# A trunk kernel on one core: a product moved inside each pair, one copy removed, stores moved to another queue

## The chip, the core and the metric

The kernel runs on one core of a Trainium2 chip. TensorE multiplies, VectorE and ScalarE work on tiles, GpSimd computes little here and issues DMAs, and SyncE only issues DMAs. Each engine takes its instructions from one queue in a fixed order, so an instruction that waits holds up all that stand behind it. The metric is the time of one execution in device microseconds, as a median of several.

## The reference

One layer of a decoder trunk is computed on x of 1024 positions by 1024 channels, all in float32. The parts that matter:

```
u    = layer_norm(x) * (1 + scale) + shift
proj = u @ w_in + b_in            # 1024 -> 12288 columns, split into 10 blocks
y_a  = (pool(a_v) @ pool_w) * pool_scale * silu(a_g)
y_b  = b_b * dwconv3(b_c * b_h) * silu(b_g)
h_c  = dwconv31(c_a * sigmoid(c_b))
y_c  = silu(layer_norm(h_c)) * silu(c_g)
m    = sum over k of sigmoid(merge_k) * (y_k @ w_branch[k])
out  = layer_norm(ALPHA * x + gate * (m @ w_out))
```

The pooling takes windows of 2, 4, 8 and 16 positions; dwconv31 is a causal convolution with 31 taps for each channel by itself. The layer norm of h_c runs over channels, so it needs the sum of all channel tiles.

## The kernel before

**Tiles.** Channels lie on the 128 partitions, so that a tile of 128 channels by 1024 positions is one buffer of 4 KB per partition. There are 37 such buffers (`BIG_SLOTS`), handed out by `slot()`. Each product of float32 matrices is made of three matmuls in the float32r format (`mm3`, line 134), because every operand is split into a high part (ScalarE) and a low part (VectorE). One half-tile product is 128x512.

**Jobs.** The work is a list of jobs. First come four plain jobs (two convolution tiles), then 46 pairs, each of which computes two blocks of 128 output columns together. A pair uses a scheme with seven block products in place of eight, named in `Pair.run` by their factors: A11 B11, A12 B21, S1 T1, S2 T2, S3 T3, S4 B22, A22 T4. Each has 12 matmuls. They use three PSUM banks: px takes A11 B11, then S2 T2, S3 T3 and A22 T4 on top of it, pz takes S1 T1 and then S4 B22, py takes A12 B21. In between, the content of a bank is copied or added into the results r1 and r2 by ScalarE (lines 525, 530, 534) and VectorE (528, 536, 538), and the next product into that bank waits for it. Six banks are there in all, so two pairs can be under way.

The pairs are of five kinds: `b` and `d` (branch B), `a` (pooling), `c` (convolution input), `cg` and `m` (gates, whose results are stored to DRAM). A `c` pair is put in after a fixed number of other pairs (`every`). After each job from the third on, `conv_step` issues six of the 30 taps that VectorE runs for each convolution tile (line 610); the 31st is ScalarE's start of the tile (606). When a tile h is done, it is stored, and it is added to a running sum; for the first tile the sum is a copy made by ScalarE (620).

**Merges.** Then follow 8 merge jobs z for branch B (48 matmuls each), with 4 pooling jobs among them, 8 merge jobs for branch A and 8 for branch C. A merge job needs its weights (SyncE's loads, split in lines 408 and 414), all eight y tiles of its branch (loaded by GpSimd's queue, split in 129 and 130) and a gate tile. The pooling jobs need pooled tiles (`a_load`) and produce sga tiles, which are stored as branch A's y. During the branch B merges the convolution's statistics are computed: the sum is split, the mean made, each tile is loaded again (hc), the mean is taken off, the tile is stored, and squares are added up (`c_square`). During the branch A merges branch C's y is computed from it (`c_y`) and stored. At the end comes the product with w_out and the last layer norm.

**Queues and order.** Loads of weights go through SyncE. Stores of intermediate tiles and their loads go through GpSimd's queue, as `store()` does unless it is given another queue. The order of instructions on each engine is not written out by hand, except for the start (`START`): a planner places them when the program is built, by the order of the code as priority and a model of durations. Extra edges of `after()` keep an instruction behind another in that plan.

Of the kernel before, what the change touches and what calls it, by code (L numbers as in the profile page):

```python
# [11 lines left out]
AF = mybir.ActivationFunctionType  # L12
# [7 lines left out]
NT = D // P  # L20
# [39 lines left out]
def kernel(  # L60
# [16 lines left out]
    nc = tc.nc  # L77
# [15 lines left out]
    LEFT, RIGHT = slice(0, HALF), slice(HALF, S)  # L93
    HALVES = (LEFT, RIGHT)

    def slot(name, dt=F32):
        return big.tile([P, D], dt, tag="big", name=name)
# [5 lines left out]
    def bank(name):  # L103
        return ps_main.tile([P, HALF], F32, tag="main", name=name)
# [92 lines left out]
    def vec(n, i):  # L197
        return vec_cols[:, base[n] + i : base[n] + i + 1]
# [195 lines left out]
    class Job:  # L394
# [41 lines left out]
        def run(self):  # L436
            if hasattr(self, "finished"):
                return
            if self.run_own is not None:
                self.run_own(self.w)  # L440
                return
            if not hasattr(self, "ps"):
                for k in range(NT):
                    for h in range(2):
                        self.part(k, h)
            self.after(self.ps)

    def bias(col):
        return bin_cols[:, col // P : col // P + 1]

    class Pair:
# [68 lines left out]
        def run(self):  # L520
            col1, col2 = self.cols
            px, pz = bank(f"px_{self.name}"), bank(f"pz_{self.name}")
            r1, r2 = slot(f"r1_{self.name}"), slot(f"r2_{self.name}")
            self.product(px, "A11", "B11", True)
            nc.scalar.activation(r1[:, LEFT], px, AF.Identity, bias=bias(col1))
            py = bank(f"py_{self.name}")
            self.product(py, "A12", "B21", True)
            nc.vector.tensor_add(r1[:, LEFT], py, r1[:, LEFT])
            self.product(pz, "S1", "T1", True)
            marks["pair"] = nc.scalar.activation(  # L530
                r2[:, RIGHT], pz, AF.Identity, bias=bias(col2)
            )
            self.product(px, "S2", "T2", False)
            nc.scalar.activation(r1[:, RIGHT], px, AF.Identity, bias=bias(col1))
            self.product(px, "S3", "T3", False)
            nc.vector.tensor_add(r2[:, RIGHT], px, r2[:, RIGHT])
            self.product(pz, "S4", "B22", False)
            nc.vector.tensor_add(r1[:, RIGHT], pz, r1[:, RIGHT])
            self.product(px, "A22", "T4", False)
            self.after(r1, px, r2)  # L540

    def store(dst, src, q=None):
        return (q or nc.gpsimd).dma_start(out=dst, in_=src)  # L543

    def dram_tiles(name, n):
        return [dram.tile([P, S], F32, name=f"{name}{j}") for j in range(n)]
# [15 lines left out]
    conv = {"n": 0, "sum": None}  # L562
# [36 lines left out]
    def conv_step(n):  # L599
        while n > 0 and conv_todo:  # L600
            item = conv_todo[0]
            j, g, h, s = item
            w = cfw_cols[:, (K31 - 1 - s) * NT + j : (K31 - 1 - s) * NT + j + 1]
            if s == 0:
                h = item[2] = slot(f"h{j}")
                ins = nc.scalar.activation(h, g, AF.Identity, bias=vec("cf_b", j), scale=w)  # L606
                if j == 0:
                    after(ins, marks["u"])
            else:
                nc.vector.scalar_tensor_tensor(  # L610
                    out=h[:, s:], in0=g[:, : S - s], scalar=w, in1=h[:, s:],
                    op0=ALU.mult, op1=ALU.add,
                )
                n -= 1
            item[3] = s + 1
            if s == K31 - 1:
                conv_todo.popleft()
                if conv["sum"] is None:
                    conv["sum"] = slot("hsum")
                    nc.scalar.copy(conv["sum"], h)  # L620
                else:
                    nc.vector.tensor_add(conv["sum"], conv["sum"], h)
                store(h_dram[j], h)
                conv["n"] += 1


    y_dram = [dram_tiles(f"y{b}_dram", NT) for b in range(3)]
# [25 lines left out]
    def a_load(g):  # L653
        for ct in (2 * g, 2 * g + 1):
            pooled[ct] = load_split(f"pool{ct}", pool_dram[ct], "split")
        for ct in (2 * g, 2 * g + 1):
            sg_a[ct] = slot(f"sga{ct}")
            after(nc.gpsimd.dma_start(out=sg_a[ct], in_=sga_dram[ct]), marks["split"])

    def a_pool(g):  # L660
        def run(w):
            for o in range(2):
                ct = 2 * g + o
                ps = [bank(f"pool_ps{ct}_{h}") for h in range(2)]
                for i in range(2):
                    for h in range(2):
                        ph, pl = pooled[2 * g + i]
                        ws = slice((2 * i + o) * P, (2 * i + o + 1) * P)
                        mm3(
                            ps[h], w[:, 0, ws], w[:, 1, ws], ph[:, HALVES[h]], pl[:, HALVES[h]],  # L670
                            i == 0, i == 1,
                        )
                t = sg_a.pop(ct)
                for h in range(2):
                    nc.vector.scalar_tensor_tensor(  # L675
                        out=t[:, HALVES[h]], in0=ps[h], scalar=vec("pool_scale", ct),
                        in1=t[:, HALVES[h]], op0=ALU.mult, op1=ALU.mult,
                    )
                store(y_dram[0][ct], t)

        jobs.append(Job(f"pool{g}", pool_w[0][g], None, None, run=run))

# [81 lines left out]
    c_dram = dram_tiles("c_dram", NT)  # L764
# [5 lines left out]
    def c_square(j):  # L770
        t = c_state.pop(("h", j))
        nc.vector.tensor_sub(t, t, c_state["mean"])
        store(c_dram[j], t)
        sq = slot(f"sq{j}")
        nc.scalar.activation(sq, t, AF.Square)
        if j == 0:
            c_state["q"] = sq
        else:
            nc.vector.tensor_add(c_state["q"], c_state["q"], sq)
# [28 lines left out]
    def c_y(ct):  # L808
        n, sg = c_state.pop(("y", ct))
        nc.vector.tensor_mul(n, n, c_state["rb"])  # L810
        nc.scalar.activation(
            n, n, AF.Silu, bias=vec("cf_ln_b", ct), scale=vec("cf_ln_g", ct)
        )
        nc.vector.tensor_mul(n, n, sg)
        store(y_dram[2][ct], n)


    y, m, m_hi, m_lo, g_in = {}, {}, {}, {}, {}
# [1 line left out]
    def y_load(b, k, mark):  # L820
        y[b, k] = load_split(f"y{b}_{k}", y_dram[b][k], mark)
# [35 lines left out]
    for b in (1, 0, 2):  # L857
        for i in range(NT // 2):
            light.append(
                lambda b=b, i=i: gates(  # L860
                    f"m{b}_{i}", C_M + b * D + 2 * i * P, AF.Sigmoid, g_dram[b][2 * i : 2 * i + 2],
                    nc.sync if (b, i) == (2, NT // 2 - 1) else None,
                )
            )
    heavy = [f for group in todo for f in group]
# [5 lines left out]
            order.append(light[li])  # L871
            li += 1
    order += light[li:]
    every = 6
    j = CLASSIC // 2
    for n, f in enumerate(order):
        if n % every == every - 1 and j < NT:
# [4 lines left out]
    n_proj = len(jobs)  # L882
# [14 lines left out]
    for op in LOADS.split():  # L897
        what, n = op[0], int(op[1:])
# [73 lines left out]
    for i, job in enumerate(jobs):  # L972
        ahead(i)
        if i >= n_proj and job.early is not None:
            job.early()
        job.run()
        if i == n_proj - 1:
            for k in range(NT):
                y_load(1, k, "pair")
        if i >= 2:  # L980
            conv_step(TAPS if i < n_proj - 1 else NT * K31)
        for f, args in hooks.get(i, ()):
            f(*args)
        if 8 <= i < 8 + NT:
            gate_row(i - 8)
        if n_proj <= i < n_proj + 8 and (i - n_proj) % 2 == 0:
            a_load((i - n_proj) // 2)
        if i == n_a - 2:
            marks["y0"] = marks["split"]
            for k in range(NT):  # L990
                y_load(0, k, "y0")
        if i == n_c - 2:
            marks["y2"] = marks["split"]
            for k in range(NT):
                y_load(2, k, "y2")
        if i == n_jobs - 3:
            gate_load()
            for d in range(NT - 2):
                m_hi[d], m_lo[d] = split_slots(f"m{d}", m[d])
        if i >= n_jobs - 2:  # L1000
            d = i - n_jobs + NT
            m_hi[d], m_lo[d] = split_slots(f"m{d}", m[d])
        if i >= n_jobs - 3:
            for k in ((0, 1), (2, 3, 4), (5, 6, 7))[i - n_jobs + 3]:
                wout_prep(k)
# [5 lines left out]
    for i in range(NT):  # L1011
# [4 lines left out]
        n = D // parts  # L1016
# [7 lines left out]
        for q, k in order:  # L1024
# [5 lines left out]
            if k == NT - 1:  # L1030
                t = slot(f"og{i}_{q}")[:, :n]
# [50 lines left out]
```

## Time and profile before

| what | value |
|---|---|
| median of 3 runs | 1385.55 us (1384.88 to 1387.03) |
| the profiled execution | 1386.24 us |
| its span, first to last instruction | 1384.5 us |
| mean granted TensorE clock in it | 0.986 |
| matmuls | 5893 |
| DMA, mean over the span | 136 GB/s |

The clock is the share of full speed that TensorE was granted. In the profile's rows a number like L134 is a line of the kernel, DVE is VectorE, ACT ScalarE, PE TensorE, POOL GpSimd, and SPq SyncE's queue. In a timeline each row has the start in us from the span's start, the duration in us, the engine, the line, what is written from what, and in brackets how long the engine was idle before it and what ended that. A row of a stretch has, for TensorE, its weight loads, VectorE, ScalarE and GpSimd, the busy time and in parentheses the number of instructions that began in it.

### The profile page before, as it was taken

To read this page: it belongs to the slowest core of one execution; us is meant where nothing else is said; L and a number is where in the kernel's file an instruction comes from. 1 tells how busy PE (TensorE), PEld (TensorE's weight loads), DVE (VectorE), ACT (ScalarE), POOL (GpSimd) and SP (SyncE) were. 2 spreads that over 40 slices of the span, in tenths; PEclk is the share of its full clock that TensorE was granted. 3 is DMA by queue.
4 is the path that set the end of the run, shared out by engine and by line. 5 is a ranking of instruction groups with operands and counts; after the bars stand their busy time and mean duration, and the time that the engine had idled before them with its cause. 6 is when DMAs were issued, how large, how long until landed. Compare 5 with 4: busy or idle time off the path is not lost. (4 is left out here: it accounts for less than half of the span.)

```text
span 1384.5 us, 15237 instructions
## 1 busy us (share of the span) xinstructions
PE 1330.3 (96%) x5893; PEld 1097.3 (79%) x5893; DVE 1099.0 (79%) x1292; ACT 527.5 (38%) x652; POOL 113.0 (8%) x220
## 2 busy tenths in 40 slices
PE   4999799999999999999999999999897999999997
PEld 3778688887888888888888888888685888888886
DVE  7999999999999589958975998699645657645576
ACT  6554244434443444435343543444422333313100
POOL 2000000000000000000000000000212232200010
PEclk9999999999999999999999999999998999999999
DMA  9511323443222313222342234224868979712332
GB/s 320 158 46 47 106 76 94 131 126 107 65 88 95 104 46 108 98 69 79 111 146 77 76 119 139 92 84 137 311 227 281 341 274 335 273 61 77 122 107 92
DMA packets 167949, 188.40 MB, mean 136 GB/s; under 512 B 6292, under 2 KB 138820, under 8 KB 167876
## 3 DMA queue, kind: packets, MB, share of 16 engines
q1 hardware_dynamic: 141936, 94.91, 23.1%
q0 software_dynamic: 25408, 92.29, 17.9%
q8 instruction: 46, 0.75, 0.2%
q10 hardware_dynamic: 532, 0.22, 0.1%
q14 instruction: 27, 0.22, 0.0%
HBM read 137.06 MB, written 50.34 MB: 135 GB/s over the span
## 5 line engine op out<-in xcount | busy, mean ns | idle before, releaser
L610 DVE SCALAR_TENSOR_TENSOR h<-r_c,cfw_cols,h 128x1023 f32<-128x1023 f32 (+9 forms) x180 | 226.9, 1261 | 5.5 <-ACT h L606 5.3
L610 DVE SCALAR_TENSOR_TENSOR h<-cs,cfw_cols,h 128x1023 f32<-128x1023 f32 (+29 forms) x60 | 75.8, 1263 | 1.3 <-ACT h L606 1.0
L832 DVE TENSOR_TENSOR g<-ps_z,g 128x512 f32<-128x512 f32 x48 | 31.7, 687 | 51.6 <-PE ps_z L134 51.1
L408 ACT ACTIVATE w_z<-raw_z 128x1024 fp32r<-128x1024 f32 x24 | 25.2, 1060 | 124.3 <-PE ps_z L134 62.3
L134 PE MATMUL ps_p<-u,w_p 128*128 128x512 f32 x192 | 48.8, 409 | 0.6 <-DVE u L346 0.6
L134 PEld LDWEIGHTS ps_p<-u,w_p 128*128 128x128 f32 x192 | 36.8, 196 | 8.8 <-DVE u L346 1.7
L414 DVE TENSOR_TENSOR w_z<-raw_z,w_z 128x1024 fp32r<-128x1024 f32 x24 | 29.1, 1220 | 14.6 <-ACT w_z L408 14.6
L543 POOL DMA_DIRECT2D g_dram<-r_m x22 | 11.7, 532 | 349.4 <-ACT r_m L718 238.1
L134 PE MATMUL py_m<-u,wa_m 128*128 128x512 f32 x144 | 36.2, 389 | 0.0
L134 PE MATMUL ps_z<-y_3h,w_z 128*128 128x512 f32 x96 | 34.0, 391 | 1.7 <-ACT y_3h L129 1.7
L134 PE MATMUL ps_z<-y_0h,w_z 128*128 128x512 f32 x96 | 35.4, 403 | 0.0
L134 PE MATMUL px_m<-u,wa_m 128*128 128x512 f32 x144 | 34.8, 389 | 0.0
L134 PE MATMUL pz_m<-u,wc_m 128*128 128x512 f32 x144 | 34.6, 389 | 0.0
L134 PE MATMUL ps_z<-y_1h,w_z 128*128 128x512 f32 x96 | 34.0, 389 | 0.0
L134 PE MATMUL ps_z<-y_2h,w_z 128*128 128x512 f32 x96 | 33.8, 389 | 0.0
L134 PE MATMUL ps_z<-y_4h,w_z 128*128 128x512 f32 x96 | 33.5, 389 | 0.0
L134 PE MATMUL ps_z<-y_7h,w_z 128*128 128x512 f32 x96 | 33.3, 389 | 0.0
L134 PE MATMUL ps_z<-y_6h,w_z 128*128 128x512 f32 x96 | 33.3, 389 | 0.0
L134 PE MATMUL ps_z<-y_5h,w_z 128*128 128x512 f32 x96 | 33.3, 389 | 0.0
L1032 DVE TENSOR_TENSOR og<-out_ps,gate_b 128x512 f32<-128x512 f32 (+1 forms) x18 | 11.1, 624 | 26.7 <-PE out_ps L134 13.4
L134 PE MATMUL px_m<-t_1h,wb_m 128*128 128x512 f32 x96 | 32.1, 389 | 0.0
L134 PE MATMUL pz_m<-t_0h,wb_m 128*128 128x512 f32 x96 | 31.5, 389 | 0.0
(567 smaller groups left out, 3879.7 us busy)
## 6 DMA issues: line engine op xcount, KB each, us to landing
raw_m<-in_w_in_dram SPq DMA_DIRECT2D x24, 512.0 KB, 4.0
raw_z<-in_w_branch_dram SPq DMA_DIRECT2D x24, 512.0 KB, 10.3
g<-g_dram POOLq DMA_DIRECT2D x24, 512.0 KB, 8.2
g_dram<-r_m POOLq DMA_DIRECT2D x22, 512.0 KB, 3.6
ada<-in_w_ada_dram SPq DMA_DIRECT2D x32, 256.0 KB, 6.4
raw_b<-in_w_in_dram SPq DMA_DIRECT2D x16, 512.0 KB, 4.0
raw_d<-in_w_in_dram SPq DMA_DIRECT2D x16, 512.0 KB, 4.0
raw_a<-in_w_in_dram SPq DMA_DIRECT2D x16, 512.0 KB, 4.0
```

Source lines behind the costliest of these rows:

```text
L134: nc.tensor.matmul(ps, w, r, start=start and n == 0, stop=stop and n == 2, skip_group_check=True)
L408: nc.scalar.activation(self.w[:, 0, : self.width], raw, AF.Identity)
L414: marks["split"] = nc.vector.tensor_tensor(out=lo, in0=raw, in1=f32(hi), op=ALU.subtract)
L543: return (q or nc.gpsimd).dma_start(out=dst, in_=src)
L610: nc.vector.scalar_tensor_tensor(out=h[:, s:], in0=g[:, : S - s], scalar=w, in1=h[:, s:], op0=ALU.mult, op1=ALU.add,)
L832: nc.vector.tensor_mul(g[:, HALVES[h]], ps[h], g[:, HALVES[h]])
L1032: nc.vector.tensor_mul(t, ps[q], final["gate"][:, sl])
```

## The change

S1 T1 moves behind S2 T2 in each pair, with its eviction. The first convolution tile becomes the running sum itself, without a copy. The stores of the branch A and branch C y tiles and of the centred convolution tiles go to SyncE's queue, on which the weights are loaded, and so do those of one more gate pair (the last two pairs of the last branch in place of the last one). A `c` pair comes after every fifth place in the list instead of every sixth. Each group of pooled tiles is requested one job earlier.

```
-            self.product(pz, "S1", "T1", True)
-            marks["pair"] = nc.scalar.activation(
-                r2[:, RIGHT], pz, AF.Identity, bias=bias(col2)
-            )
             self.product(px, "S2", "T2", False)
             nc.scalar.activation(r1[:, RIGHT], px, AF.Identity, bias=bias(col1))
+            self.product(pz, "S1", "T1", True)
+            marks["pair"] = nc.scalar.activation(
+                r2[:, RIGHT], pz, AF.Identity, bias=bias(col2)
+            )
             self.product(px, "S3", "T3", False)
...
                 if conv["sum"] is None:
-                    conv["sum"] = slot("hsum")
-                    nc.scalar.copy(conv["sum"], h)
+                    conv["sum"] = h
...
-                store(y_dram[0][ct], t)
+                store(y_dram[0][ct], t, nc.sync)
...
-        store(c_dram[j], t)
+        store(c_dram[j], t, nc.sync)
...
-        store(y_dram[2][ct], n)
+        store(y_dram[2][ct], n, nc.sync)
...
-                    nc.sync if (b, i) == (2, NT // 2 - 1) else None,
+                    nc.sync if b == 2 and i >= NT // 2 - 2 else None,
...
-    every = 6
+    every = 5
...
-        if n_proj <= i < n_proj + 8 and (i - n_proj) % 2 == 0:
-            a_load((i - n_proj) // 2)
+        if n_proj - 1 <= i < n_proj + 7 and (i - n_proj) % 2 == 1:
+            a_load((i - n_proj + 1) // 2)
```

Here `n_proj` is the number of jobs before the merges, 50.

More of the change, by code (lines that the diff above doesn't have):

```diff
@@ L528, in run @@
             nc.vector.tensor_add(r1[:, LEFT], py, r1[:, LEFT])
+            self.product(px, "S2", "T2", False)
+            nc.scalar.activation(r1[:, RIGHT], px, AF.Identity, bias=bias(col1))
             self.product(pz, "S1", "T1", True)
@@ L532, in run @@
             )
-            self.product(px, "S2", "T2", False)
-            nc.scalar.activation(r1[:, RIGHT], px, AF.Identity, bias=bias(col1))
             self.product(px, "S3", "T3", False)
```

## The prediction

> **What bounds the kernel now.** I read the page first, for which engine is the bound, then the waits of TensorE, then stretches of equal length, which price a wait together with what follows it.
>
> ```profile
> span 1384.5 us, 15237 instructions
> PE 1330.3 (96%) x5893; PEld 1097.3 (79%) x5893; DVE 1099.0 (79%) x1292; ACT 527.5 (38%) x652; POOL 113.0 (8%) x220
> ```
>
> TensorE is the bound. Only time in which it stands still, or runs at a lower clock, can be won, and no matmul is added or removed. The profiled execution took 1386.24 us for this span. These are its waits from 60 us to 1375 us (line waited for, total, times, longest):
>
> ```profile
> PE pool_ps L134 <- ACT pool6h L129: 10.2, 1, 10.2
> PE px_b L134 <- ACT r_b L525: 5.6, 1, 5.6
> PE pz_d L134 <- DVE wb_d L508: 2.4, 1, 2.4
> PE pool_ps L134 <- ACT pool0h L129: 1.7, 1, 1.7
> PE ps_z L134 <- ACT y_3h L129: 1.7, 1, 1.7
> PE px_b L134 <- DVE wc_b L508: 1.4, 1, 1.4
> PE ps_z L134 <- DVE y_3l L130: 0.5, 1, 0.5
> ```
>
> That is the whole list: 23.5 us, in four places. Stretches show more than the waits, because matmuls after a wait are slower (busy us and count of each engine, then the granted clock, the DMA share and GB/s):
>
> ```profile
> 160.00:180.00 20.00, 11.97 (x37) 8.88 (x37) 17.05 (x17) 7.19 (x9) 0.53 (x1) 0.74 0.16 63
> 180.00:200.00 20.00, 20.00 (x90) 16.57 (x89) 19.98 (x23) 5.61 (x7) 0.00 (x0) 1.00 0.14 35
> 200.00:300.00 100.00, 100.00 (x443) 82.81 (x442) 96.47 (x103) 44.95 (x55) 3.19 (x6) 1.00 0.39 120
> 400.00:500.00 100.00, 100.00 (x443) 82.84 (x442) 77.54 (x86) 44.63 (x54) 3.19 (x6) 1.00 0.29 93
> 980.00:1000.00 20.00, 16.06 (x58) 11.17 (x57) 12.04 (x12) 9.97 (x11) 3.17 (x6) 0.91 1.02 389
> 1040.00:1060.00 20.00, 9.83 (x40) 7.81 (x39) 10.13 (x11) 4.14 (x5) 6.04 (x12) 0.78 0.79 257
> 1060.00:1080.00 20.00, 20.00 (x86) 16.47 (x86) 13.85 (x15) 7.09 (x7) 4.50 (x9) 0.97 0.87 302
> ```
>
> A full stretch of 20 us starts 90 matmuls, 0.222 us each. The stretch at 160 starts 37: 53 missing, **11.8 us** (place A). At 980 there are 58: 32 missing, **7.1 us** (place C). At 1040 and 1060 there are 40 and 86: 54 missing, **12.0 us** (place D). The 1.4 us for wc_b, in the first pair, is place B. A, C and D together, 30.9 us, are all that this change could win outside B.
>
> **The change part by part.**
>
> *The running sum.* Place A, on ScalarE and TensorE:
>
> ```profile
> 171.86 1.04 ACT L620 COPY hsum<-h 128x1024 f32<-128x1024 f32 x1 [9.87 <-DVE h L610]
> 172.81 0.68 ACT L525 ACTIVATE r_b<-px_b,bin_cols 128x512 f32<-128x512 f32 x1
> 173.54 0.79 PE L134 MATMUL px_b<-t_1h,wb_b 128*128 128x512 f32 x1 [5.63 <-ACT r_b L525]
> ```
>
> The copy stands in ScalarE's queue and waits 9.87 us for the last tap of the first convolution tile. Behind it stands the eviction that S2 T2 of that pair (px_b<-t_1h) needs, so TensorE waits 5.63 us and ends 0.05 us after that eviction. The 2.4 us for wb_d just before it hang on the same knot: the held S2 T2 keeps its weights, so the next pair's arrive late. The change deletes the copy (1.04 us of ScalarE, which is free) and lets the tile itself be the sum; nothing else on ScalarE then waits for a tap. The addition of the second tile now also waits for the first tile's store, which goes out when that tile ends, 30 taps earlier: no cost. Gain at most 11.8 us, at least 0: VectorE ran its late taps during the stall (17.05 us busy of 20) and has only 0.02 + 3.53 us free from 180 to 300. If TensorE no longer pauses, taps fall further behind, and taps are the one VectorE work that TensorE does not wait for. I take 9.8, leaving 2 us for a split or eviction that comes late behind taps.
>
> *A c pair after every five others.* A convolution tile is 30 taps on VectorE, six per job, so five jobs. With one pair in seven jobs the chain starves, which is the hole in VectorE's row at 400 to 500 (77.54 against 96.47). With one in six it starves at one job only, and by the order the code builds, the last tile ends with job 42 of jobs 0 to 49 instead of in the last one. The number of taps is unchanged. It costs nothing by itself where TensorE was fully busy beside a VectorE at 96.47 of 100 us, which the row at 200 shows; without that cover it is the second rival. What it brings is at place C, on GpSimd's queue:
>
> ```profile
> 959.46 0.54 POOL L734 DMA_DIRECT2D y_0l<-y_dram  x1
> ...
> 971.49 0.54 POOL L543 DMA_DIRECT2D g_dram<-r_m  x1 [10.96 <-ACT r_m L557]
> 972.01 0.53 POOL L734 DMA_DIRECT2D y_2l<-y_dram  x1
> 975.10 0.54 POOL L543 DMA_DIRECT2D h_dram<-h  x1 [2.56 <-DVE h L610]
> 975.63 0.53 POOL L734 DMA_DIRECT2D y_3l<-y_dram  x1
> ...
> 985.85 0.73 PE L134 MATMUL ps_z<-y_3h,w_z 128*128 128x512 f32 x2 [1.67 <-ACT y_3h L129]
> ```
>
> The loads of the first merge's input stand behind a gate store (10.96 us waiting) and behind the last tile's store. The change takes away both: the third gate pair's two stores of the last branch move to the weight queue, and the last tile is done seven jobs sooner (84 matmuls each at 0.226 us, 133 us). y_2 can then be issued up to 11 us sooner and y_3 up to 3 us more than that. Both ends: 7.1 us if buffers are free as early as the queue, 0 if a buffer is what they wait for, since the pairs' operands hold most of the 37 buffers until the last products. The load of y_0 went out at 959, 16 us before the queue let y_3 go, so buffers do come free early: I take 5.5. The first pooling load now stands ahead of the first gate load, so that gate lands up to four loads later; its product waits in a bank, of which there are six: no cost.
>
> *Stores on the weight queue, pooling loads one job sooner.* Place D, on GpSimd's queue:
>
> ```profile
> 1044.40 0.54 POOL L543 DMA_DIRECT2D y_dram<-sga  x1 [13.01 <-DVE sga L675]
> 1046.25 1.05 POOL L768 DMA_DIRECT2D hc<-h_dram  x2
> 1047.29 0.53 POOL L734 DMA_DIRECT2D pool6l<-pool_dram  x1
> 1057.19 1.06 ACT L129 ACTIVATE pool6h<-pool6l 128x1024 fp32r<-128x1024 f32 x1 [7.94 <-DMA pool6l<-pool_dram]
> ```
>
> pool6l was issued behind two stores that waited for VectorE and behind two loads of convolution tiles, then took 9.9 us to land. In the changed code neither stands ahead of it: those stores are SyncE's, and the request comes one job sooner, before the hc loads. The queue stood idle from 1031.4 (1044.40 less 13.01); the load may go then, if its buffer is free. By the code I count 36 of 37 buffers then: 16 for y_1, 5 gate tiles, 12 for two pooling groups, 3 for the sum and its halves. Issued by 1037 it lands by 1047, where TensorE began to wait. Gain between 3.3 us (if it only takes the place of the first of these rows, 1047.29 against 1044.0, and lands as slowly) and 12.0; I take 10.9.
>
> What the 24 stores plus two gate stores cost on SyncE is the time for which weight loads stand behind a waiting store:
>
> ```profile
> POOL y_dram L543 <- DVE sga L675: 47.5, 6, 19.8
> 1012.58 0.37 SPq L386 DMA_DIRECT2D raw_z<-in_w_branch_dram  x1
> 1044.05 1.06 ACT L408 ACTIVATE w_z<-raw_z 128x1024 fp32r<-128x1024 f32 x1 [6.33 <-PE pool_ps L134]
> raw_z<-in_w_branch_dram SPq DMA_DIRECT2D x24, 512.0 KB, 10.3
> ```
>
> The weight load at 1012.58 is for the fifth merge job, whose split starts at 1044.05: 31.5 us, of which 10.3 to land, so 21 us in hand. The longest wait in the store's row was 19.8 us. I take 0; the upper end is the excess over 21 us.
>
> *The order inside a pair.* S3 T3 adds to the bank that S2 T2 leaves, so it must wait for an eviction; S1 T1 is moved between them as cover, 12 matmuls:
>
> ```profile
> 119.71 0.39 PE L134 MATMUL px_d<-t_1h,wb_d 128*128 128x512 f32 x1
> 119.94 2.88 PE L134 MATMUL pz_d<-u,wc_d 128*128 128x512 f32 x12
> 121.10 0.67 ACT L534 ACTIVATE r_d<-px_d,bin_cols 128x512 f32<-128x512 f32 x1
> 126.06 0.39 PE L134 MATMUL px_d<-t_0h,wc_d 128*128 128x512 f32 x1
> ```
>
> S2 T2 ends at 120.1, its eviction at 121.8, and S3 T3 starts at 126.1, 4.3 us later: the planner already filled that time with S4 B22 and the next pair. No wait of this kind is in the list of waits. I take 0; place B (1.4 us, waiting for a weight split) stays.
>
> **The sum.** 9.8 + 5.5 + 10.9 = 26.2 us. 1386.24 - 26.2 = 1360.0 for an execution like the profiled one; that lies 0.7 above the median of 1385.55, so **1359.4**. If everything is won, 1385.55 - 30.9 - 1.4 = 1353.3.
>
> **The rivals.**
>
> *First: place D shrinks but stays.* For it: the DMA share is 0.79 and 0.87 in the two stretches of D and 1.02 at 980, so a load that is issued sooner meets others. If only 3.3 of the 12.0 us come back, the time is 1359.4 + 7.6 = 1367.0. Against it: between the pooling loads the queue stood still for 13.01 us, so there is room for a load to be moved into. [...]
>
> *Second: VectorE becomes the bound.* For it: 19.98 of 20 us at 180, 96.47 at 200, and the hole at 400 to 500 in which it could catch up is filled by the c pairs. If TensorE has to wait for all that VectorE did during the stall of A, the 9.8 us are lost: 1369.2. Against it: 443 matmuls in 100 us beside 96.47 of VectorE.
>
> *Third: no change.* The gaps only mark where other late work would show next, and new waits of the same size come up: within 2.7 us of 1385.55.
>
> *Fourth, slower: the pair becomes too tight.* With S1 T1 as cover the planner needs less of the next pair as filler, so A22 T4 can follow S4 B22 directly. It needs VectorE's addition after S3 T3:
>
> ```profile
> 103.39 0.39 PE L134 MATMUL px_b<-t_0h,wc_b 128*128 128x512 f32 x1
> 105.90 0.68 DVE L536 TENSOR_TENSOR r_b<-px_b,r_b 128x512 f32<-128x512 f32 x1
> 111.09 0.39 PE L134 MATMUL px_b<-t_1h,wd_b 128*128 128x512 f32 x1
> ```
>
> S3 T3 ended at 103.8 and the addition at 106.6, 2.8 us, against 2.7 us of cover by one product (119.94 to 122.66). With one more tap ahead of it (1.26 us) that is 1.3 us of waiting in each of 46 pairs, 60 us: 1359.4 + 60 = 1419. It decides from 0.57 us a pair, where the 26.2 us are used up. Against it: now there are 4.5 us between the addition and A22 T4 (106.6 to 111.1), left by the same planner.
>
> **How the numbers follow.** Forecast 0.62 (its own range 1353 to 1365), first rival 0.12, second 0.11, no change 0.05, slower 0.10. A measurement of this kernel can tell about 0.2%, 2.8 us, from no change. Faster is the first three, 0.85; within 0.2% 0.05; slower 0.10. The range goes from everything won, 1353, past the second rival with some of the first, to 1375; what it leaves out is the last two cases.
>
> **What would show it.** Right: no line for r_b or pool6h in TensorE's waits; 88 to 90 matmuls in each 20 us from 160 to 1300; VectorE's hole at 400 to 500 gone and the last tap near 840 us; y_2l directly behind y_1l on GpSimd's queue and pool6l before the hc loads; still about zero waits on px and pz banks. Wrong: a wait on weight splits between 160 and 440 (second rival), on pool6h or pool7h (first), many short waits of px products (fourth), or weight loads that land after their split could start.

## The result and the profile after

The changed kernel takes **1360.84 us** (median of 4, 1360.64 to 1361.05); the kernel before took 1386.29 us beside it (1384.88 to 1387.30). The ratio is 0.9817, with a 95% interval from 0.9800 to 0.9834: 25.4 us or 1.8% faster. The forecast was 1359.4. The profiled execution took 1360.99 us, 25.25 us less than the profiled one of before, and all numbers below are read against that.

First the head of the page of the changed kernel:

```profile
span 1359.1 us, 15236 instructions
PE 1324.8 (97%) x5893; PEld 1093.2 (80%) x5893; DVE 1097.5 (81%) x1292; ACT 531.0 (39%) x653; POOL 99.3 (7%) x194
```

The same 5893 matmuls are there, and TensorE is still the bound. Next, all waits of TensorE in the changed kernel from 60 us to 1375 us (line waited for, total, times, longest):

```profile
PE px_b L134 <- DVE wc_b L508: 1.9, 1, 1.9
PE pool_ps L134 <- ACT pool0h L129: 1.7, 1, 1.7
PE px_a L134 <- DVE wa_a L508: 0.8, 1, 0.8
PE px_a L134 <- ACT r_a L525: 0.8, 1, 0.8
PE px_m L134 <- ACT r_m L525: 0.6, 1, 0.6
PE ps_z L134 <- ACT y_3h L129: 0.3, 1, 0.3
PE px_c L134 <- DVE wa_c L508: 0.3, 1, 0.3
```

23.5 us of waits have become 6.4. The 10.2 us for pool6h, the 5.6 us for r_b and the 2.4 us for wb_d are gone. In their place stand four short waits of pairs (wa_a, r_a, r_m, wa_c), 2.5 us in all, that were not there before. The stretches of the changed kernel show what these are worth (columns as in the prediction):

```profile
160.00:180.00 20.00, 20.00 (x90) 16.55 (x89) 20.00 (x22) 7.87 (x11) 0.00 (x0) 1.00 0.19 48
180.00:200.00 20.00, 20.00 (x90) 16.55 (x89) 20.00 (x22) 9.90 (x12) 0.00 (x0) 1.00 0.21 61
400.00:500.00 100.00, 100.00 (x443) 82.77 (x442) 94.25 (x102) 43.91 (x54) 3.19 (x6) 1.00 0.27 85
800.00:900.00 100.00, 99.23 (x439) 81.85 (x438) 87.19 (x104) 43.18 (x63) 6.37 (x12) 1.00 0.36 116
920.00:940.00 20.00, 19.37 (x86) 15.72 (x85) 14.34 (x19) 9.79 (x13) 1.06 (x2) 1.00 0.39 132
980.00:1000.00 20.00, 18.24 (x80) 14.44 (x79) 11.27 (x13) 5.49 (x6) 2.00 (x4) 1.00 0.95 338
1040.00:1060.00 20.00, 20.00 (x90) 16.57 (x89) 14.04 (x15) 6.39 (x6) 3.16 (x6) 1.00 1.00 344
1060.00:1080.00 20.00, 20.00 (x90) 16.53 (x90) 13.47 (x15) 7.22 (x7) 1.05 (x2) 1.00 0.68 238
```

At 160 TensorE starts 90 matmuls where it started 37, beside a VectorE that is busy for every one of 40 us. The hole in VectorE's row at 400 to 500 is filled (94.25 against 77.54). At 980 there are 80 matmuls instead of 58, and at 1040 and 1060 none is missing, at a DMA share of 1.00 in the first of the two. The stretch from 920 to 940, full before, now has 86. GpSimd's queue in the changed kernel (a timeline):

```profile
945.17 0.54 POOL L733 DMA_DIRECT2D y_1l<-y_dram  x1
950.42 0.53 POOL L733 DMA_DIRECT2D y_2l<-y_dram  x1 [4.71 <-DMA g_dram<-r_m]
950.94 0.53 POOL L733 DMA_DIRECT2D y_3l<-y_dram  x1
...
993.10 0.53 POOL L733 DMA_DIRECT2D pool6l<-pool_dram  x1
1004.15 0.53 POOL L733 DMA_DIRECT2D pool7l<-pool_dram  x1 [10.53 <-DMA y_dram<-sga]
...
1017.38 0.53 POOL L767 DMA_DIRECT2D hc<-h_dram  x1 [8.95 <-DMA y_dram<-sga]
```

No store stands between these loads. pool6l goes out at 993.10, 54 us sooner than before, and ahead of the hc loads. Where the queue waits in these rows, it waits for a store that has to land, as in the 4.71 us before y_2l; I read that as a buffer that comes free.

### The profile page after: what moved, and what is told of

Its sections match the earlier page's. It is cut to its first block, busy times and chain, and to the rows that moved or that the text cites. A ratio compares the mean times of both kernels' runs of the same rounds, so it can differ in the third digit from the quotient of the medians.

```text
span 1359.1 us, 15236 instructions
## 1 busy us (share of the span) xinstructions
PE 1324.8 (97%) x5893; PEld 1093.2 (80%) x5893; DVE 1097.5 (81%) x1292; ACT 531.0 (39%) x653; POOL 99.3 (7%) x194
## 5 line engine op out<-in xcount | busy, mean ns | idle before, releaser
L610 DVE SCALAR_TENSOR_TENSOR h<-r_c,cfw_cols,h 128x1017 f32<-128x1017 f32 (+12 forms) x180 | 227.6, 1266 | 1.9 <-ACT h L606 1.5
L408 ACT ACTIVATE w_z<-raw_z 128x1024 fp32r<-128x1024 f32 x24 | 25.3, 1062 | 129.7 <-PE ps_z L134 77.4
L134 PEld LDWEIGHTS px_m<-u,wa_m 128*128 128x128 f32 x144 | 27.0, 188 | 5.6
L134 PEld LDWEIGHTS pz_m<-u,wc_m 128*128 128x128 f32 x144 | 27.0, 188 | 5.6
```

The source lines that it names most:

```text
L134: nc.tensor.matmul(ps, w, r, start=start and n == 0, stop=stop and n == 2, skip_group_check=True)
L408: nc.scalar.activation(self.w[:, 0, : self.width], raw, AF.Identity)
L610: nc.vector.scalar_tensor_tensor(out=h[:, s:], in0=g[:, : S - s], scalar=w, in1=h[:, s:], op0=ALU.mult, op1=ALU.add,)
```

## The experiments

To compare traces I count missing matmuls. A full stretch of 20 us has 89 or 90; what is short of 90 in the stretches between 160 and 1080 us is counted by place (A is 160 to 200, C 960 to 1000, D 1020 to 1080), and under "new" stands what is short elsewhere where the kernel before was full (the stretch at 320, with 85 in the kernel before too, counts only for what is below that). A missing matmul is taken as 0.222 us. That is slightly low: a stretch's count takes in matmuls that run across its edges (68 stretches of 20 us of the changed kernel add up to 6011 of its 5893), and 443 in 100 us make 0.226 us each, by which the 24.9 us of the next table would be 25.3. Times are medians with, beside each, the kernel before of the same set (1387.14, 1388.11 or 1386.84 us).

```
kernel                             A    C    D  new   us less by trace   us less measured
before                            53   32   54    0
changed                            0   10    0   17   24.9               25.4
e1  only the running sum           0   23   50    0   14.7               14.3
e2  only the pair order           53   11   46   13    3.6                3.1
e3  only c after every fifth      54   18   32    0    7.8                7.0
e4  only stores and early loads   55   18    0    0   14.7               15.7
e5  only the stores               55   17   18    0   10.9               14.1
e6  only the early loads          55   28    0    0   12.4               10.8
e7  changed, old pair order        0   13    0    0   28.0               31.4
e8  changed, c after every sixth   0   34    0   13   20.4               24.3
e9  changed, again                 0   11    0   17   24.6               24.5
e10 changed, old pair order again  0   13    0    0   28.0               29.3
e11 changed, with the copy        54   12    0   14   13.1               13.6
e12 changed, 8 taps a job          3    3    0   94    8.7               10.0
```

The count explains each time to within 4 us, mostly within 2. Each row is read on its own below.

**e1, the running sum alone.**

```diff
-                    conv["sum"] = slot("hsum")
-                    nc.scalar.copy(conv["sum"], h)
+                    conv["sum"] = h
```

> The kernel before with the running sum alone (no copy of the first convolution tile). If the copy's place in ScalarE's queue makes the stall at 160 to 180 us (place A), the waits of TensorE for r_b (5.6 us) and wb_d (2.4 us) go, and the time falls by 9 to 12 us to about 1375; the stalls at 980 to 1000 and 1047 to 1058 stay. If the stall is VectorE's lateness and the copy only shows it, TensorE waits for VectorE's splits between 160 and 300 instead, and the time falls by less than 3 us.

Measured: 1372.80 us, ratio 0.9900 (0.9883 to 0.9916). Stretches of this kernel:

```profile
160.00:180.00 20.00, 20.00 (x90) 16.57 (x89) 20.00 (x21) 6.70 (x9) 0.00 (x0) 1.00 0.20 67
960.00:980.00 20.00, 18.46 (x77) 13.60 (x75) 14.71 (x14) 12.01 (x14) 7.85 (x15) 1.00 0.93 335
980.00:1000.00 20.00, 18.29 (x80) 14.60 (x80) 10.46 (x12) 4.67 (x6) 3.69 (x7) 1.00 0.67 246
1020.00:1040.00 20.00, 14.55 (x65) 11.68 (x63) 10.04 (x11) 5.09 (x6) 3.17 (x6) 0.95 0.79 270
1040.00:1060.00 20.00, 17.32 (x65) 14.07 (x66) 11.54 (x12) 7.09 (x7) 6.61 (x13) 0.79 0.83 303
```

Place A is won whole (53 to 0, 11.8 us): the copy was its cause, and VectorE, full for 20 of 20 us here, gives nothing back. Place D starts 13.6 us sooner and stays nearly as large (50 for 54). C falls from 32 to 23, though nothing was done to the queues there: a new plan moves the late places too. That is why 14.3 us came off and not 9 to 12.

**e2, the pair order alone.**

```diff
+            self.product(px, "S2", "T2", False)
+            nc.scalar.activation(r1[:, RIGHT], px, AF.Identity, bias=bias(col1))
             self.product(pz, "S1", "T1", True)
...
-            self.product(px, "S2", "T2", False)
-            nc.scalar.activation(r1[:, RIGHT], px, AF.Identity, bias=bias(col1))
```

> The kernel before with S1 T1 behind S2 T2 alone. If the planner had already filled the gap between S2 T2 and S3 T3, the time changes by less than 2 us, places A, C and D stay as they are. If the order inside a pair makes pairs too tight, many short waits for px banks come up and the time grows by 10 us or more. If it frees something that the waits do not show, the time falls by more than 3 us.

Measured: 1384.05 us, ratio 0.9979 (0.9970 to 0.9989). Two of the waits of TensorE in this kernel are new:

```profile
PE px_m L134 <- DVE wa_m L508: 1.6, 2, 1.0
PE px_a L134 <- ACT r_a L525: 0.5, 1, 0.5
```

They cost 13 matmuls. The gain of 3.1 us comes from C (32 to 11) and D (54 to 46), 6.4 us together by the table, not from the pairs, where there was nothing to win. So the time moved by more than the 2 us expected, and C and D did not stay as they were.

**e3, a c pair after every fifth other pair, alone.**

```diff
-    every = 6
+    every = 5
```

> The kernel before with a c pair after every fifth place alone. By the prediction this takes the last tile's store out of the way of y_3 and gives part of place C: 1 to 4 us less, with the copy's stall of place A still there. If VectorE is the bound once its hole at 400 to 500 us is filled, TensorE waits for weight splits between 200 and 800 and the time grows.

Measured: 1380.15 us, ratio 0.9947 (0.9933 to 0.9962). VectorE's hole at 400 to 500 is filled (96.56 of 100 us busy) without a new wait in the pairs. C falls to 18, and D to 32: 3.1 and 4.9 us. The 1 to 4 us expected were for C alone; that D would shrink was not foreseen.

**e4, the stores on SyncE's queue and the early pooling loads; e5, the stores alone; e6, the early loads alone.** e4 has both parts of this diff, e5 all but the last, e6 the last.

```diff
-                store(y_dram[0][ct], t)
+                store(y_dram[0][ct], t, nc.sync)
...
-        store(c_dram[j], t)
+        store(c_dram[j], t, nc.sync)
...
-        store(y_dram[2][ct], n)
+        store(y_dram[2][ct], n, nc.sync)
...
-                    nc.sync if (b, i) == (2, NT // 2 - 1) else None,
+                    nc.sync if b == 2 and i >= NT // 2 - 2 else None,
...
-        if n_proj <= i < n_proj + 8 and (i - n_proj) % 2 == 0:
-            a_load((i - n_proj) // 2)
+        if n_proj - 1 <= i < n_proj + 7 and (i - n_proj) % 2 == 1:
+            a_load((i - n_proj + 1) // 2)
```

> The kernel before with the stores on the weight queue and the pooling loads one job sooner, and nothing else. If the waiting of GpSimd's queue made the stall for pool6h, it goes and the time falls by 9 to 13 us (place D, with some of C from the gate pair's stores) to about 1375. [...]

> The kernel before with the stores on the weight queue alone; the pooling loads are requested where they were. If the two stores ahead of pool6l on GpSimd's queue made the stall for pool6h, TensorE's wait for it (10.2 us before) falls to 3 us or less and the time to about 1374. If the place of the request (behind the hc loads) made it, the wait stays at 6 us or more and the time stays above 1380. If DMA sharing made it, also 6 us or more.

> The kernel before with the pooling loads requested one job sooner, stores left on GpSimd's queue. If the place of the request made the stall for pool6h, the wait goes to 3 us or less here and the time falls to about 1375; if the stores ahead of it made it, the wait stays at 6 us or more.

Measured: e4 1371.45 us, ratio 0.9886 (0.9871 to 0.9901); e5 1374.05, 0.9903 (0.9888 to 0.9918); e6 1377.31, 0.9927 (0.9910 to 0.9943). In e4 and e6 no wait for pool6h is left; in e5 this remains, of the waits of TensorE:

```profile
PE pool_ps L134 <- ACT pool6h L129: 2.1, 1, 2.1
```

And GpSimd's queue in e6, where the stores still stand on it:

```profile
1020.07 0.54 POOL L543 DMA_DIRECT2D y_dram<-sga  x1 [9.51 <-DVE sga L675]
...
1024.03 0.53 POOL L734 DMA_DIRECT2D pool6l<-pool_dram  x1
1036.39 0.54 POOL L543 DMA_DIRECT2D y_dram<-sga  x1 [11.83 <-DVE sga L675]
```

The early request stands behind a store that waits 9.51 us, but ahead of the one that waits 11.83 us, and that is enough. So place D had two remedies, each nearly sufficient by itself: the request one job sooner (54 to 0 missing) or a queue without waiting stores (54 to 18). The stores help C as well (32 to 17; the early loads leave it at 28), so e4's 15.7 us lie above the 9 to 13 expected. In none of the three does TensorE wait for weights of a merge, so the stores cost SyncE's queue nothing that shows.

**e7 and e10, the changed kernel with the old pair order; e9, the changed kernel again beside e10.** e2's diff taken back.

> The changed kernel with S1 T1 back ahead of S2 T2. If the order inside a pair is worth nothing, 1359 to 1363, and the four short waits of the changed kernel for wa_a, r_a, r_m and wa_c (2.5 us in all) may go with it. If the order gives what it gave alone (3.1 us), 1364.

> The changed kernel itself, beside the next run on the same chip. Theory (moving S1 T1 between S2 T2 and S3 T3 costs about 4 us in the changed kernel): 1360 to 1361.5 us, and the next run 3 to 5 us below it. Rival (the 4 us lie between two chips or two sessions): the two within 1 us of each other.

> The changed kernel with S1 T1 back ahead of S2 T2, everything else changed. Theory: 1356 to 1357.5 us, with only the waits for wc_b (1.9) and pool0h (1.7) left on TensorE. Rival: 1360 to 1361, the same as the changed kernel beside it.

Measured: e7 **1356.72 us** (1356.51 to 1357.12), ratio 0.9775 (0.9760 to 0.9789); e9 1362.32 (1360.59 to 1362.52), 0.9820 (0.9805 to 0.9835); e10 1357.58 (1356.47 to 1359.51), 0.9790 (0.9775 to 0.9805). Side by side on one chip the old order is 4.7 us faster, and the two sets of times do not overlap. All waits of TensorE in e7 from 60 to 1375 us:

```profile
PE px_b L134 <- DVE wc_b L508: 1.9, 1, 1.9
PE pool_ps L134 <- ACT pool0h L129: 1.7, 1, 1.7
```

The four short waits of pairs are gone, and with them the 17 matmuls, 3.8 us. This version beats both kernels, and is faster than either case that was expected for it. Where such a wait comes from can be seen in the changed kernel around 864 us: in TensorE's timeline, VectorE's and ScalarE's.

```profile
850.19 2.88 PE L134 MATMUL px_a<-u,wa_a 128*128 128x512 f32 x12
...
864.71 0.50 PE L134 MATMUL px_a<-t_1h,wb_a 128*128 128x512 f32 x1 [0.77 <-ACT r_a L525]
```

```profile
862.36 1.22 DVE L638 TENSOR_TENSOR s<-s 128x1022 f32<-128x1022 f32 x1
```

```profile
863.66 0.20 ACT L637 COPY s<-s 128x4 f32<-128x4 f32 x1 [1.25 <-issue]
863.97 0.69 ACT L525 ACTIVATE r_a<-px_a,bin_cols 128x512 f32<-128x512 f32 x1
```

A11 B11 into px_a was done at 853.1. Its eviction ran only at 863.97, because a small copy of the pooling windows stands ahead of it on ScalarE and needs, by the code, a sum of VectorE that ended at 863.58 (the profile itself names nothing for the copy's 1.25 us). S2 T2 waits for that eviction. In e10, with the old order, the same knot is there (ScalarE, then TensorE):

```profile
856.67 0.19 ACT L637 COPY s<-s 128x4 f32<-128x4 f32 x1 [0.40 <-DVE s L638]
856.77 0.68 ACT L525 ACTIVATE r_a<-px_a,bin_cols 128x512 f32<-128x512 f32 x1
```

```profile
862.49 0.39 PE L134 MATMUL px_a<-t_1h,wb_a 128*128 128x512 f32 x1
```

But there S2 T2 starts 5.0 us after the eviction has ended (862.49 less 857.46), and nothing is lost. That is no chance of one pair. From the two timelines I took, for each of the 46 pairs, the time from the end of this eviction to the start of S2 T2. Its median is 7.26 us before and 7.27 in e7, with the old order, and 4.55 in the changed kernel: 2.7 us less, the length of one product (2.72 us from 119.94 to 122.66 in the prediction's rows). Some evictions come late with either order, up to 14.6 us after their product. In the changed kernel two of them, r_a and r_m, reach TensorE (0.05 and 0.06 us from eviction to S2 T2). The 2.7 us alone don't make these two waits. In e10 the same two pairs have their evictions 5.0 and 2.8 us after the product and 5.0 and 4.5 us in hand; in the changed kernel the evictions come 10.9 and 10.8 us after the product. So the plan with the new order also runs these evictions later, and 2.7 us less would by itself have left about 2 us in hand. Both follow from the order; no run parts them. The other two waits are for splits of weights (wa_a, wa_c), and 8 of the 17 matmuls are missing in their stretches (640 and 260); what makes them was not tried by itself.

**e8, the changed kernel with a c pair after every sixth.** e3's diff taken back.

> The changed kernel with a c pair after every sixth place again. If the c pairs' place frees GpSimd's queue for the y loads, place C comes back in part: waits for y_3 and the like at 970 us, 1363 to 1366, with the last tap near 950 us. If the stores alone did that, within 1.5 us of the changed kernel.

Measured: 1363.83 us (1361.24 to 1365.03), ratio 0.9823 (0.9809 to 0.9838). VectorE's hole is back (84.51 at 400 to 500), and C grows from 10 to 34. By that count the kernel should lose 5.3 us to C and win 0.9 in the pairs. By its median it is 3.0 us above the changed kernel's 1360.84 and 1.5 above e9, and its ratio is the changed kernel's within the intervals. The direction is shown by the trace, the size by time is not.

**e11, the changed kernel with the copy kept.** e1's diff taken back.

> The changed kernel with the copy of the first convolution tile kept. Theory (the copy, waiting for the last tap, blocks the eviction that S2 T2 needs): the stall between 160 and 180 us is back, with r_b or another eviction of that pair in TensorE's waits at 4 to 7 us, and the time is 9 to 14 us above the changed kernel: 1370 to 1375. The shorter cover of S2 T2 in the new order would put the stall earlier, not make it go away. Rival (with the new order and the denser c pairs the queue has other work to do at that time): under 3 us above, 1361 to 1364.

Measured: 1373.26 us (1372.12 to 1374.43), ratio 0.9900 (0.9883 to 0.9916), 10.9 us above e9 beside it. ScalarE's timeline:

```profile
173.80 1.04 ACT L620 COPY hsum<-h 128x1024 f32<-128x1024 f32 x1 [9.88 <-DVE h L610]
174.75 0.68 ACT L525 ACTIVATE r_b<-px_b,bin_cols 128x512 f32<-128x512 f32 x1
```

The stall is back as it was (9.87 us then, 9.88 now), with no other place changed by more than 3 matmuls. In the whole change the running sum is worth 10.9 us.

**e12, the changed kernel with eight taps a job.**

```diff
-TAPS = 6
+TAPS = 8
```

> The changed kernel with eight taps per job in place of six, so that the same taps ask for more of VectorE while they last and are done sooner. The second rival of the prediction in a stronger form: if VectorE's taps delay splits and evictions as soon as it has no free time, TensorE waits for splits (wa, wb, wc, wd) between 160 and 800 us and the time rises by 5 to 40 us, 1366 to 1400. If taps can fall behind without holding anything up, VectorE stays full, TensorE's waits stay under 10 us, and the time is within 2 us of the changed kernel.

Measured: 1376.85 us (1375.45 to 1378.24), ratio 0.9928 (0.9913 to 0.9942), 14.5 us above e9. Stretches, then a row of ScalarE and one of TensorE, of this kernel:

```profile
220.00:240.00 20.00, 16.06 (x63) 12.40 (x61) 20.00 (x22) 8.06 (x10) 1.59 (x3) 0.91 0.43 141
...
260.00:280.00 20.00, 18.16 (x79) 14.41 (x79) 20.00 (x21) 5.23 (x7) 0.00 (x0) 1.00 0.28 81
```

```profile
222.36 0.69 ACT L525 ACTIVATE r_cg<-px_cg,bin_cols 128x512 f32<-128x512 f32 x1 [0.67 <-DVE r_d L705]
...
232.36 0.69 ACT L525 ACTIVATE r_b<-px_b,bin_cols 128x512 f32<-128x512 f32 x1 [3.01 <-DVE h L610]
```

```profile
223.10 0.50 PE L134 MATMUL px_cg<-t_1h,wb_cg 128*128 128x512 f32 x1 [2.56 <-ACT r_cg L525]
```

VectorE is full for 20 of 20 us and now TensorE does wait: evictions on ScalarE wait for VectorE's rows (0.67 us for r_cg, 3.01 us for r_b, there a tap), and S2 T2 waits 2.56 us for the first of the two. So taps are free to fall behind only up to a point; six a job lie short of it (e7 has no wait of this kind) and eight beyond, with the new pair order. With the old one eight were not tried. I had expected the waits to be for splits of weights. They are mostly for evictions: the two longest entries are r_cg, 3.8 us, and r_b, 1.8 us.

## Why the prediction was right, point by point

**The bound and the ceiling** held. Everything won lies in TensorE's stalls, and the places priced at 30.9 us gave 53 + 22 + 54 = 129 matmuls, 28.7 us. New short waits took 17 matmuls back, 3.8 us: 24.9 by the count, 25.25 by the profiled executions, 26.2 forecast. The total is close in part because two errors lie on opposite sides.

**Place A, taken at 9.8 of 11.8.** Mechanism and place as predicted. It gave 11.8 by the count in e1 and 10.9 as a difference of times in e11. The 2 us held back for splits late behind taps were not needed there. That nothing else on ScalarE would wait for a tap did not hold as the profile has it: between 100 and 300 us one split waits 2.7 us for a tap in the changed kernel (wc_d), and two evictions 2.1 and 0.7 us in e7, without a wait of TensorE behind them. e1's 14.3 us are more than place A because the new plan also made C and D smaller.

**Place C, taken at 5.5 of 7.1.** It gave 22 matmuls, 4.9 us. That a buffer might hold the loads was right for y_2l (4.71 us), which therefore does not follow y_1l directly, as I had said it would. What stays is almost all one wait that stood in my list and got no account: 1.7 us for pool0h, the same in every kernel run here. ScalarE's and TensorE's timelines of the changed kernel:

```profile
964.48 0.62 ACT L408 ACTIVATE w_pool<-raw_pool 128x512 fp32r<-128x512 f32 x1
...
983.28 0.63 ACT L408 ACTIVATE w_pool<-raw_pool 128x512 fp32r<-128x512 f32 x1 [4.67 <-issue]
983.82 1.04 ACT L129 ACTIVATE pool0h<-pool0l 128x1024 fp32r<-128x1024 f32 x1
```

```profile
982.81 0.39 PE L134 MATMUL ps_z<-y_7h,w_z 128*128 128x512 f32 x1
```

pool0l was requested at 965.3 and took 5.2 us, so it lay ready for 13 us; ScalarE was idle for 4.67 us and then split pooling weights and the tile. No queue of loads was in the way. The weights split at 983.28 are not those of pool0h, which were split at 964.48, but the next pooling job's, and they stand ahead of pool0h on ScalarE. Three weights have been split before them (958.45, 964.48, 969.38), the code has three buffers for them (`W8_BUFS`), and the last matmul that reads the first ends at 983.20. So pool0h very likely waits behind a split that waits for a buffer, the knot of place A once more; no run takes it away.

**Place D, taken at 10.9 of 12.0.** It gave all 54 matmuls, 12.0 us. I had charged it to both edits as one; e5 and e6 show that either would have done most of it. The step on SyncE's queue held: no merge weight is waited for.

**The order inside a pair, taken at 0: wrong.** This is the step that failed. I looked at the wait that S1 T1 was to cover, found it already covered (4.3 us of slack), and set no cost. I did not ask what S1 T1 had covered where it stood: the eviction of A11 B11 ahead of S2 T2. Moving it takes 2.7 us of cover from S2 T2 in the median pair, the plan that comes of it runs some evictions and splits later, and the whole costs 4.7 us in the changed kernel (e10 against e9). The fourth rival was the right kind of mechanism at the wrong product: no wait for A22 T4 appears, but two for S2 T2, in two pairs of 46 and not in all.

**The rivals.** The first falls: at a DMA share of 1.00 from 1040 to 1060 TensorE starts 90 matmuls and waits for no load. Nor is it borne out by e5, in which nothing but the queue of stores changes: it is 14.1 us faster, and what it takes away is time behind waiting stores (10.2 us of waiting for pool6h before, 2.1 in e5). The second falls at six taps (A: 90 matmuls beside 20.00 of 20 us of VectorE) and is real at eight; a trace of it is there at six, the 0.3 us for the split wa_c at 270, which e7 does not have. The third falls by the interval.

**The signs that I named.** Right: no r_b, no pool6h, the hole filled, pool6l ahead of hc. Wrong: the last tap starts after 854 us instead of about 840, since the taps lag; four short waits on px products, one of them for a weight split between 160 and 440, as I had named for the second rival; and 85 to 87 matmuls in four stretches (260, 640, 860, 920) besides the 80 at 980.

**Why parts don't add.** Alone the four parts save 14.3 + 3.1 + 7.0 + 15.7 = 40.1 us, together 25. By the table they take 4 + 8 + 22 + 54 = 88 matmuls from place D, which holds 54, and 9 + 21 + 14 + 14 = 58 from C, which gives 22. Any change of the plan shifts these late places, and each is counted once when all are made.

## What to carry to other kernels

Before work is moved to cover one wait, find the wait that it covers now: in this kernel the covered one was the smaller (nothing before the move) and the uncovered one cost 4.7 us. An instruction that waited was priced here by what stood behind it on its engine, so look there for evictions (ScalarE) and loads (GpSimd) first: a copy of 1.04 us that waited 9.87 us, with an eviction behind it, was worth 10.9 us, and stores, one of which waited 13.01 us, stood ahead of a load for which TensorE waited 10.2 us. When parts are tried alone, count the loss by place, since two remedies of one place both look worth it and are paid once.

## What I had not expected

In these traces a wait cost more than its length, and short ones no less per us than long ones. The four short waits of pairs, 2.5 us, took 3.8 us of matmuls; 5.6 + 2.4 us at place A before took 11.8, and 10.2 us at place D took 12.0. What differs is the granted clock: 1.00 in each stretch shown of the changed kernel (920: 0.63 us of waiting, 4 matmuls or 0.9 us), 0.74 at place A. Two waits of nearly one length differ in it. TensorE in e12:

```profile
240.40 0.50 PE L134 MATMUL px_b<-t_0h,wc_b 128*128 128x512 f32 x1 [1.77 <-ACT r_b L530]
...
242.00 1.06 PE L134 MATMUL px_b<-t_0h,wc_b 128*128 128x512 f32 x2
242.86 0.63 PE L134 MATMUL px_b<-t_0l,wc_b 128*128 128x512 f32 x1
```

After a wait of 1.77 us two matmuls take 0.86 us from start to start, 0.43 each against 0.226, and the granted clock from 240 to 244 us is 0.66; the 1.7 us for pool0h leave it at 1.00. So matmuls start 1.9 times as far apart after the first of these waits; what lowers the clock there and not after the second, no run shows.

The plan as a whole answers to every edit: removing one copy at 172 us changed place C at 980 us from 32 to 23 missing matmuls, and the pair order alone took it to 11, with none of the stores or loads there touched by hand.
